# A feed forward block computed plainly in two of its four blocks and by Strassen's algorithm in the others

## Chip, core and metric

The kernel runs on one core of a Trainium2 chip. The metric is the device time of one execution in microseconds; the median of three runs before the change is 1663.09 us (1661.41 to 1663.12).

## What is computed

One inference step of a two-layer recurrent decoder over 576 tokens (512 of a prompt, 64 of samples), width 1024. Each layer has a mixer, a feed forward and a gated embedding:

```python
for i in range(DEPTH):                       # 2 layers
    hn = rmsnorm(h, prm['norm_mix'][i])
    ...                                      # layer 0: mLSTM and retention; layer 1: HGRN2 and S5
    h = h + out
    hn = rmsnorm(h, prm['norm_ff'][i])
    h = h + jnp.matmul(jnp.square(jax.nn.relu(jnp.matmul(hn, prm['w_ff1'][i]))), prm['w_ff2'][i])
    gate = jax.nn.sigmoid(jnp.matmul(rmsnorm(h, prm['norm_ple'][i]), prm['w_ple_gate'][i]))
    h = h + gate * jnp.matmul(p[i], prm['w_ple_proj'][i])
```

The feed forward goes from 1024 to 4096 features and back. The state space model (S5) of the second layer needs constants that depend on its parameters alone: powers of its poles, turned phases, and products of these with its input and output matrices. They can be made at any time before the second layer.

## The kernel before

Features lie on the 128 partitions and the 576 tokens along the free dimension, in two halves of 288 columns (HALF). All matrices are float32. TensorE takes each product in three: a value is split into a high part (rounded to fp32r) and a low part (the rest), and high x high, high x low and low x high are added in PSUM. So a weight of 128 x 128 against 576 tokens takes six matmuls of 288 columns. `unit` loads eight such weights (512 KB) by SP's queue, ScalarE copies the high part (L238) and VectorE subtracts it for the low part (L239); the raw, high and low tiles have two buffers each. `cols` runs the 48 matmuls of one unit into a PSUM bank pair, of which three rotate (`pb`, L250).

`ff` is the feed forward, once for each layer. It goes over four blocks of 1024 hidden features. In a block, the first product (called FF1 below) takes eight units; each result is scaled and cut at zero by VectorE (`fu`, L562) and squared by ScalarE (L563). The second product, from the block's 1024 features to all 1024 outputs, is done with Strassen's algorithm: `seven` takes two outputs n and n+1 and the two token halves as a 2 x 2 problem and makes seven products of 4 x 3 = 12 matmuls in place of eight (L519), so 84 matmuls for each of four pairs. `seven_in` makes the sums of u that this needs (seven splits of 288 columns and four sums for each pair of u), `seven_weights` the sums of weights (four sums, L493 to L501, and seven splits of 512 columns, L480 and L481). Two PSUM banks accumulate on through several products: after each product VectorE adds the bank as it stands to h (L524), and the next product into that bank has to wait for this.

In the first feed forward alone, `s5_hooks` hangs the work on the constants of S5 beside the loop. `hook(b, part, n)` runs what is planned for block b, first (0) or second (1) product, step n. The tables (`s5_tables`, many small VectorE instructions on 128 x 32 to 128 x 288) come from (0,0,4) on. Then come 24 steps, three for each of eight sets of four groups: `elem` (six multiplications and additions on VectorE, L1263 to L1265, with two loads of s5bc), `prod` (four transposes, L1277, and four products, L1279, on TensorE, then small DMAs to DRAM) and `s5_turn` (some 40 small VectorE instructions on s5R, then stores of s5R and s5M). s5R and the product tile s5t of `elem` share one buffer. The first step stands at (0,1,6), the last at (3,1,0). All run at a lowered priority (`LATE`).

The order of each engine's queue is not that of the code: a planner with a timeline model places the instructions in the order of priority as their inputs and buffers come free. The engines then run their queues in that fixed order.

Of the kernel before, what the change touches and what calls it, by code (L numbers as in the profile page):

```python
# [10 lines left out]
F32R = mybir.dt.float32r  # L11
AF = mybir.ActivationFunctionType
ALU = mybir.AluOpType
# [3 lines left out]
P = 128  # L17
# [3 lines left out]
HALF = NT // 2  # L21
# [8 lines left out]
LOP = "fqig"  # L30
MAGIC = 12582912.0
LATE = 100

# [140 lines left out]
class K:  # L176
# [364 lines left out]
    def ff(self, l, hooks=None):  # L541
        nc = self.nc
        xs, r = self.norm(f"ff{l}")
        with ExitStack() as st:
            pool = lambda name, bufs: st.enter_context(self.tc.tile_pool(name=f"{name}{l}", bufs=bufs))

            ap, fw = pool("fa", 3), pool("fw", 1)
            todo = hooks(st) if hooks else {}
            up = pool("ff", 4)

            def hook(*at):
                if at in todo:
                    todo[at]()

            for b in range(4):
                us, pair = [], []
                for n in range(8):
                    hook(b, 0, n)
                    w = self.unit("col", "w_ff1", l, (8 * b + n) * P, 0)
                    ps = self.cols(w, xs)  # L560
                    u = self.np_.tile([P, NT], F32, name="fu", tag=("sqa", "sq")[n % 2])
                    nc.vector.scalar_tensor_tensor(self.sv(u), self.pv(ps), 0.0, self.sv(r()), ALU.max, ALU.mult)  # L562
                    nc.scalar.activation(u, u, AF.Square)  # L563
                    if n % 2 == 0:
                        pair = [u]
                        parts = self.seven_in(pair, up, ap)
                        us.append(next(parts))
                    else:
                        pair.append(u)
                        next(parts)  # L570
                if b == 3 and l == 1:
                    self.embed_in(l, self.np_, nc.sync, self.xp, "sq")
                for n in range(0, 8, 2):
                    hook(b, 1, n)
                    hook(b, 1, n + 1)
                    self.seven(l, n, b, us, fw)


    def ple(self, l):
# [646 lines left out]
    def s5_hooks(self, st):  # L1226


        nc = self.nc
# [70 lines left out]
        def late(f, *at):  # L1300

            def run():
                with self.tc.high_priority(-LATE):
                    f()
            old = hooks.get(at)
            hooks[at] = run if old is None else lambda: (old(), run())

        for j in range(4, 13):
            late(piece, 0, j // 8, j % 8)
        late(lambda: piece(99), 0, 1, 5)  # L1310
        at = lambda i: (i // 16, i // 8 % 2, i % 8)
        steps = [lambda f=f, ct=ct, q=q: f(ct, q) for ct in range(4) for q in range(2)
                 for f in (elem, prod, lambda ct, q: self.s5_turn(sp, ct, q))]
        for i, f in enumerate(steps):
            late(f, *at(14 + i * 44 // len(steps)))
        return hooks


# [421 lines left out]
```

## Time and profile before

| | |
|---|---|
| median of three runs | 1663.09 us |
| the profiled execution, its own time | 1658.75 us |
| its span, first to last instruction | 1656.5 us |
| TensorE (PE) busy | 1563.3 us, 94% |
| VectorE (DVE) busy | 1261.0 us, 76% |
| ScalarE (ACT) busy | 718.1 us, 43% |
| GpSimd (POOL) busy | 214.5 us, 13% |

The trace is of one execution. PE counts matmuls, PEld weight loads, which overlap them; a matmul's end is modelled, so that neighbours overlap and the pace is read from starts. [...] A row of waits names who waited, for whom, the sum in us, the number of waits and the longest. In a row of the timeline the number in brackets is the engine's idle time just before, and what ended it. In a row of instruction groups the numbers behind the bar are busy us in all, mean ns of one, and idle us before them.

### The profile page before, as it was taken

The page shows a single profiled execution, that of the slowest core. Times are in us where ns is not written, and L with a number is a line of the kernel's source. Part 1 is how long each engine was busy: PE and PEld are TensorE (multiplying, and loading weights), DVE is VectorE, ACT ScalarE, POOL GpSimd, SP SyncE. Part 2 cuts the span into 40 slices and gives each one's busy share as a digit, 9 for nine tenths or more (in the row PEclk, how much of TensorE's full clock was granted, in tenths as well). Part 3 has the DMA queues.
Part 4 walks back from the last instruction along what each step waited for, and adds up shares of the span by engine and source line. Part 5 has one row for each costly group of instructions (what it writes and reads, how often), then busy time and mean ns, then how long its engine had stood idle before and what let it go on. Part 6 is the DMA issues. An engine that isn't in the chain of part 4 may idle for free.

```text
span 1656.5 us, 30820 instructions
## 1 busy us (share of the span) xinstructions
PE 1563.3 (94%) x12213; PEld 1502.4 (91%) x12213; DVE 1261.0 (76%) x2745; ACT 718.1 (43%) x1326; POOL 214.5 (13%) x204
## 2 busy tenths in 40 slices
PE   7999999999999999999899788989999999999896
PEld 6989789999999899899899787979999999999895
DVE  6977666658998988989685896386777785867855
ACT  4333222335534435345453356374543534435553
POOL 1311122201000000000023465231100000000000
PEclk9999999999999999999999899899999999999998
DMA  7222222223232333332326422521223222222221
GB/s 266 99 91 81 94 78 92 82 95 103 71 120 97 103 129 103 120 121 84 133 91 179 142 93 79 153 87 70 89 77 115 77 75 96 81 95 91 90 77 58
DMA packets 83311, 168.83 MB, mean 102 GB/s; under 512 B 33760, under 2 KB 40800, under 8 KB 83040
## 3 DMA queue, kind: packets, MB, share of 16 engines
q1 hardware_dynamic: 81512, 163.40, 29.9%
q8 instruction: 96, 1.57, 0.4%
q0 software_dynamic: 640, 2.36, 0.4%
q10 hardware_dynamic: 1016, 1.11, 0.2%
q14 instruction: 47, 0.39, 0.1%
HBM read 142.70 MB, written 24.13 MB: 101 GB/s over the span
## 4 chain that ended last, share of the span: by engine, by line
PE 71%; DVE 17%; DMA 4%; ACT 3%; issue 3%; SPq 1%; POOL 0%; DVEq 0%; ACTq 0%
PE pb L250 49%; PE pb L519 13%; PE pm L519 2%; DMA wr<-in_w_dram 2%; DVE h L524 1%; DVE wl L239 1%; DVE wsl L481 1%; DVE xl L286 1%; DVE wl L481 1%; PE pm L653 1%; DVE ul L283 1%; PE pm L1005 1%; DVE e L1526 1%; PE pm L891 1%; DMA sG<-Gd 1%
## 5 line engine op out<-in xcount | busy, mean ns | idle before, releaser
L250 PE MATMUL pb<-xh,wh 128*128 128x288 f32 x2480 | 550.8, 301 | 28.4 <-ACT xh L282 6.3
L250 PE MATMUL pb<-xh,wl 128*128 128x288 f32 x2480 | 547.5, 299 | 0.5 <-DVE wl L239 0.5
L250 PE MATMUL pb<-xl,wh 128*128 128x288 f32 x2480 | 547.6, 299 | 0.1
L250 PEld LDWEIGHTS pb<-xh,wh 128*128 128x128 f32 x2480 | 406.8, 191 | 36.7 <-issue 10.7
L250 PEld LDWEIGHTS pb<-xl,wh 128*128 128x128 f32 x2480 | 406.9, 191 | 7.8 <-issue 7.0
L250 PEld LDWEIGHTS pb<-xh,wl 128*128 128x128 f32 x2480 | 406.5, 191 | 6.0 <-issue 4.8
L238 ACT CAST wh<-wr 128x1024 fp32r<-128x1024 f32 x155 | 162.2, 1048 | 312.4 <-PE pb L250 254.4
L239 DVE TENSOR_TENSOR wl<-wr,wh 128x1024 fp32r<-128x1024 f32 x135 | 166.1, 1231 | 28.2 <-ACT wh L238 25.0
L519 PE MATMUL pb<-uh,wsh 128*128 128x288 f32 x512 | 154.7, 302 | 12.9 <-DVE h L524 9.9
L519 PE MATMUL pb<-ul,wsh 128*128 128x288 f32 x512 | 152.1, 297 | 0.0
L519 PE MATMUL pb<-uh,wsl 128*128 128x288 f32 x512 | 151.0, 297 | 0.0
L480 ACT CAST wsh<-wsum 128x512 fp32r<-128x512 f32 x128 | 78.9, 619 | 145.0 <-PE pb L519 99.2
L519 PEld LDWEIGHTS pb<-uh,wsh 128*128 128x128 f32 x512 | 96.8, 189 | 19.3 <-DVE h L524 11.1
L524 DVE TENSOR_TENSOR h<-h,pb 128x288 f32<-128x288 f32 x192 | 85.2, 447 | 32.1 <-PE pb L519 31.5
L519 PEld LDWEIGHTS pb<-ul,wsh 128*128 128x128 f32 x512 | 96.9, 189 | 0.0
L519 PEld LDWEIGHTS pb<-uh,wsl 128*128 128x128 f32 x512 | 96.7, 190 | 0.0
L481 DVE TENSOR_TENSOR wsl<-wsum,wsh 128x512 fp32r<-128x512 f32 x128 | 87.4, 683 | 2.3 <-ACT wsh L480 1.1
L562 DVE SCALAR_TENSOR_TENSOR fu<-pb,r 128x576 f32<-128x576 f32 x64 | 48.1, 753 | 46.0 <-PE pb L250 45.9
L282 ACT CAST uh<-ut 128x288 fp32r<-128x288 f32 x128 | 52.6, 431 | 45.2 <-DVE ut L453 24.9
L411 POOL TENSOR_TENSOR sqa<-sqa,sq 128x576 f32<-128x576 f32 x3 | 5.1, 1714 | 441.7 <-ACT sq L410 441.7
L239 POOL TENSOR_TENSOR wl<-wr,wh 128x1024 fp32r<-128x1024 f32 x20 | 50.5, 2529 | 90.2 <-ACT wh L238 88.6
L1507 POOL MEMSET W<- 128x576 f32 x4 | 2.3, 576 | 429.5 <-PE pb L519 428.1
(495 smaller groups left out, 2563.2 us busy)
## 6 DMA issues: line engine op xcount, KB each, us to landing
wr<-in_w_dram SPq DMA_DIRECT2D x219, 512.0 KB, 3.7
sR<-Rd SPq DMA_DIRECT2D x12, 256.0 KB, 2.9
h<-in_hT_dram SPq DMA_DIRECT2D x8, 288.0 KB, 5.2
prd<-po POOLq DMA_DIRECT2D x8, 288.0 KB, 3.2
Gd<-s5G SPq DMA_DIRECT2D x8, 288.0 KB, 3.8
prj<-prd SPq DMA_DIRECT2D x8, 288.0 KB, 4.6
sG<-Gd SPq DMA_DIRECT2D x8, 288.0 KB, 5.4
s_in<-in_Cst_dram SPq DMA_DIRECT2D x4, 516.0 KB, 7.9
```

Source lines behind the costliest of these rows:

```text
L238: nc.scalar.copy(hi, raw)
L239: (nc.gpsimd if self.lo_pool else nc.vector).tensor_tensor(lo, raw, hi.bitcast(F32), ALU.subtract)
L250: mm(ps[:, j if bank is None else bank, :HALF], a, b[:, j * HALF:(j + 1) * HALF], start=first and a is wh and b is xh, stop=last and a is wl)
L282: nc.scalar.copy(hi, src)
L283: nc.vector.tensor_tensor(lo, src, hi.bitcast(F32), ALU.subtract)
L286: nc.vector.scalar_tensor_tensor(lo, src, scale, hi.bitcast(F32), ALU.mult, ALU.subtract)
L480: nc.scalar.copy(hi, src)
L481: nc.vector.tensor_tensor(lo, src, hi.bitcast(F32), ALU.subtract)
L519: mm(ps, a[:, k], x[:, i], start=start and k == 0 and a is wh and x is xh, stop=k == 3 and a is wl, skip_group_check=not start)
L524: nc.vector.tensor_tensor(o, o, ps, ALU.add)
L562: nc.vector.scalar_tensor_tensor(self.sv(u), self.pv(ps), 0.0, self.sv(r()), ALU.max, ALU.mult)
L653: nc.tensor.transpose(dst, src[:n, t0:t0 + tn], self.ident[:n, :n])
```

## The change

The first feed forward takes two kinds of blocks. In the first two (NPLAIN) the second product is done plainly: u is split whole (576 columns) as the inputs of the first product are, `w_ff2` is taken in eight units of 48 matmuls by `cols`, and VectorE adds each result to its h whole. The two other blocks, and the second feed forward, keep Strassen's algorithm. The 24 steps of the constants are hung closer: over 21 steps of the loop instead of 44, from (0,1,6) to (2,0,2).

```diff
+NPLAIN = 2
...
             for b in range(4):
                 us, pair = [], []
+                plain = l == 0 and b < NPLAIN
...
                     nc.scalar.activation(u, u, AF.Square)
-                    if n % 2 == 0:
+                    if plain:
+                        if n % 2 == 0:
+                            hi, lo = (up.tile([P, 7, HALF], F32R, name=t, tag=t) for t in ("uh", "ul"))
+                        f = lambda t: t[:, n % 2 * 2:n % 2 * 2 + 2].rearrange("p a b -> p (a b)")
+                        us.append((f(hi), f(lo)))
+                        self.split_into(*us[-1], u)
+                    elif n % 2 == 0:
                         pair = [u]
...
                     hook(b, 1, n + 1)
-                    self.seven(l, n, b, us, fw)
+                    if not plain:
+                        self.seven(l, n, b, us, fw)
+                        continue
+                    for m in (n, n + 1):
+                        w = self.unit("col", "w_ff2", l, m * P, 8 * b)
+                        ps = self.cols(w, us)
+                        nc.vector.tensor_tensor(self.sv(self.h[m]), self.sv(self.h[m]), self.pv(ps), ALU.add)
...
-            late(f, *at(14 + i * 44 // len(steps)))
+            late(f, *at(14 + i * 21 // len(steps)))
```

Lines of the changed kernel stand 1 to 14 further down (L250 is L251, L1277 is L1291, L1264 is L1278, L1218 is L1232; the plain product's add is L590).

TensorE's queue where the first block's second product begins, before. `uh`, `ul` are the parts of u, `wh`, `wl` those of the weights, `pb` and `pm` PSUM banks:

```order
L250 MATMUL pb<-xl,wh 128x288 x2
L250 MATMUL pb<-xh,wl 128x288 x2
L519 MATMUL pb<-uh,wh 128x288
L519 MATMUL pb<-ul,wh 128x288
L519 MATMUL pm<-uh,wh 128x288
L519 MATMUL pm<-ul,wh 128x288
L519 MATMUL pb<-uh,wl 128x288
```

The same place now:

```order
L251 MATMUL pb<-xl,wh 128x288 x2
L251 MATMUL pb<-xh,wl 128x288 x2
L251 MATMUL pb<-uh,wh 128x288 x2
L251 MATMUL pb<-ul,wh 128x288 x2
L251 MATMUL pb<-uh,wl 128x288 x2
```

Two Strassen products that shared the engine (pb and pm) have given way to the first product's own form, both halves for each weight.

VectorE's queue in the second block's second product, before, from the end of a turn (L1218 writes s5R last) to the next `elem` (L1264 writes s5t into the same buffer once s5R is stored):

```order
L1218 TENSOR_SCALAR s5R<-s5R 64x256
L524 TENSOR_TENSOR h_123<-h_123,pb 128x288
L495 TENSOR_TENSOR wsum<-wsum,wr_6556 128x512
L524 TENSOR_TENSOR h_121<-h_121,pb 128x288
L481 TENSOR_TENSOR wsl<-wsum,wsh 128x512
L1264 TENSOR_TENSOR s5t<-s5bc,s5y_5001 128x4x128
L498 TENSOR_TENSOR wsum<-wr_6556,wsum 128x512
L1265 TENSOR_TENSOR s5ET<-s5ET,s5t 128x512
```

Such a place now, in the same product:

```order
L1232 TENSOR_SCALAR s5R<-s5R 64x256
L590 TENSOR_TENSOR h_121<-h_121,pb 128x576
L240 TENSOR_TENSOR wl<-wr_6557,wh 128x1024
L1278 TENSOR_TENSOR s5t<-s5bc,s5y_4929 128x4x128
L1279 TENSOR_TENSOR s5ET<-s5ET,s5t 128x512
L1277 TENSOR_TENSOR s5G<-s5bc,s5w_4922 128x576
L590 TENSOR_TENSOR h_122<-h_122,pb 128x576
L1278 TENSOR_TENSOR s5t<-s5bc,s5w_4923 128x576
L240 TENSOR_TENSOR wl<-wr_6613,wh 128x1024
```

Between the end of a turn and the `elem` that takes its buffer stand two instructions in place of four, and the weight splits of the plain units stand behind.

TensorE's queue at a set of constants in FF1, before (the last of the eight sets):

```order
L250 MATMUL pb<-xl,wh 128x288
L1277 MATMUL pm<-cc,s5ET 128x128
L250 MATMUL pb<-xl,wh 128x288
L1277 MATMUL pm<-cc,s5ET 128x128
L250 MATMUL pb<-xh,wl 128x288
L1277 MATMUL pm<-cc,s5ET 128x128
L250 MATMUL pb<-xh,wl 128x288
L1277 MATMUL pm<-cc,s5ET 128x128
L250 MATMUL pb<-xh,wh 128x288
L1279 MATMUL pm<-s5G,s5ET 16x128
```

The last set now, in FF1 of the third block:

```order
L251 MATMUL pb<-xh,wl 128x288 x2
L251 MATMUL pb<-xh,wh 128x288 x2
L1291 MATMUL pm<-cc,s5ET 128x128 x4
L251 MATMUL pb<-xl,wh 128x288 x2
L251 MATMUL pb<-xh,wl 128x288 x2
```

Four transposes that each stood between two matmuls stand together; their four products (L1293) follow together too, 16 rows on. Of the eight sets, three now stand so; before, one stood together whole, and two with transposes alone.

## Rows read from the trace of the kernel before

**Rows 1.** The page: span, and busy time of each engine.

```profile
span 1656.5 us, 30820 instructions
...
PE 1563.3 (94%) x12213; PEld 1502.4 (91%) x12213; DVE 1261.0 (76%) x2745; ACT 718.1 (43%) x1326; POOL 214.5 (13%) x204
```

**Rows 2.** Windows, feed forward 1: length, PE, PEld, DVE, ACT, POOL busy (count), clock

```profile
388.60:439.40 50.80, 50.74 (x389) 50.77 (x390) 48.12 (x175) 28.99 (x52) 0.84 (x1) 1.00 0.35 95
388.60:504.80 116.20, 111.97 (x821) 109.25 (x822) 110.03 (x385) 50.95 (x92) 0.84 (x1) 0.99 0.33 100
504.80:612.10 107.30, 105.70 (x767) 100.37 (x766) 95.22 (x266) 44.81 (x84) 0.00 (x0) 1.00 0.34 111
612.10:722.60 110.50, 106.47 (x779) 101.75 (x779) 98.54 (x275) 48.39 (x94) 0.00 (x0) 1.00 0.35 111
722.60:819.80 97.20, 91.78 (x667) 88.27 (x665) 79.97 (x188) 45.65 (x84) 0.78 (x3) 1.00 0.28 93
```

**Rows 3.** Windows of feed forward 2: whole, a middle block, the last part.

```profile
1178.20:1575.70 397.50, 390.24 (x2908) 387.12 (x2908) 297.00 (x553) 177.65 (x311) 0.00 (x0) 1.00 0.26 88
1326.80:1423.40 96.60, 96.05 (x723) 95.82 (x722) 70.64 (x132) 40.82 (x72) 0.00 (x0) 1.00 0.26 88
1520.10:1575.70 55.60, 50.08 (x362) 47.92 (x360) 46.64 (x87) 27.29 (x46) 0.00 (x0) 1.00 0.23 79
```

**Rows 4.** Waits of PE, feed forward 1: total us, times, longest us.

```profile
PE pb L519 <- DVE h L524: 7.3, 14, 1.3
PE pb L519 <- ACT wh L480: 2.6, 4, 0.9
```

**Rows 5.** Windows of line L250 alone: length, PE, PEld busy (count), clock.

```profile
400.00:436.00 36.00, 36.00 (x280) 36.00 (x279) 1.00 0.35 95
1390.00:1420.00 30.00, 30.00 (x227) 30.00 (x226) 1.00 0.26 88
```

**Rows 6.** The constants on PE: windows of L1277 (four), then of L1279.

```profile
388.60:504.80 116.20, 0.60 (x4) 0.49 (x4) 0.99 0.33 100
504.80:612.10 107.30, 2.60 (x12) 1.61 (x12) 1.00 0.34 111
612.10:722.60 110.50, 2.61 (x12) 1.61 (x12) 1.00 0.35 111
722.60:819.80 97.20, 1.00 (x4) 0.57 (x4) 1.00 0.28 93
388.60:504.80 116.20, 0.41 (x8) 0.13 (x8) 0.99 0.33 100
504.80:612.10 107.30, 3.84 (x24) 1.12 (x24) 1.00 0.34 111
612.10:722.60 110.50, 3.26 (x25) 0.91 (x24) 1.00 0.35 111
722.60:819.80 97.20, 1.57 (x8) 0.44 (x8) 1.00 0.28 93
```

**Rows 7.** A window, and PE's timeline there: start, us, instruction.

```profile
453.50:456.90 3.40, 3.40 (x15) 3.40 (x16) 2.94 (x9) 0.62 (x1) 0.00 (x0) 0.51 0.00 0
453.33 0.45 PE L519 MATMUL pb<-uh,wsh 128*128 128x288 f32 x1 [1.34 <-DVE h L524]
453.57 0.45 PE L519 MATMUL pb<-ul,wsh 128*128 128x288 f32 x1
```

**Rows 8.** The page: costliest groups, those of a unit's weights and of u.

```profile
L238 ACT CAST wh<-wr 128x1024 fp32r<-128x1024 f32 x155 | 162.2, 1048 | 312.4 <-PE pb L250 254.4
L239 DVE TENSOR_TENSOR wl<-wr,wh 128x1024 fp32r<-128x1024 f32 x135 | 166.1, 1231 | 28.2 <-ACT wh L238 25.0
L562 DVE SCALAR_TENSOR_TENSOR fu<-pb,r 128x576 f32<-128x576 f32 x64 | 48.1, 753 | 46.0 <-PE pb L250 45.9
```

**Rows 9.** Waits of DVE, feed forward 1, for the store of s5R.

```profile
DVE s5t L1264 <- DMA Rd<-s5R: 4.5, 2, 2.8
```

**Rows 10.** The page: loads of weights, us from issue to landing.

```profile
wr<-in_w_dram SPq DMA_DIRECT2D x219, 512.0 KB, 3.7
```

## Prediction

> **What bounds the kernel now.** I read the page's first section, then windows over the stretch that the change touches, then TensorE's waits, then the prices of single instructions. TensorE is busy 1563.3 of 1656.5 us [rows 1], so an edit pays only as far as it shortens or lengthens TensorE's own queue. The stretch is the first feed forward, 388.6 to 819.8 us. Cut where the last Strassen product of each block ends, its four blocks take 116.2, 107.3, 110.5 and 97.2 us [rows 2]; up to 90 matmuls of the next block's first product are drawn in ahead of such an end, so I count matmuls by window. The second feed forward runs the same Strassen loop without the constants, and there a block takes 96.6 us [rows 3]. The reader is to see two things: VectorE is busy 110.0 of 116.2 us in the first block against 70.6 of 96.6 in the second feed forward, and TensorE's waits in the first feed forward end mostly with VectorE's adds to h (7.3 us in 14 waits) and with ScalarE's copies of Strassen's weights (2.6 us in 4) [rows 4].
>
> To split a block's time I need the matmul's pace. A window of 30.0 us without a wait counts 227 matmuls, two of which began before it: 0.1335 us each. In the first block's first product the pace is quicker, 36.0/278 = 0.130 us [rows 5].
>
> Block time = matmuls x 0.1335 + the constants' own TensorE time + the rest, which is waits, restarts after them and half clock. Counts are those of rows 2 less two at the edge and less the constants' instructions; the constants' time is the sum of their two lines [rows 6].
> - Block 0: 116.2 - 807 x 0.1335 (107.7) - 1.0 = 7.5. Since some 320 matmuls ran at 0.130 (1.1 us gained), the waits are really 8.6.
> - Block 1: 107.3 - 729 x 0.1335 (97.3) - 6.4 = 3.6.
> - Block 2: 110.5 - 741 x 0.1335 (98.9) - 5.9 = 5.7.
> - Block 3: 97.2 - 653 x 0.1335 (87.2) - 2.6 = 7.4.
> - Second feed forward, a middle block: 96.6 - 721 x 0.1335 (96.25) = 0.35; its last part, 1520.1 to 1575.7: 55.6 - 360 x 0.1335 (48.1) = 7.5 [rows 3].
>
> So the end of the last block loses 7.4 us with the constants and 7.5 without. That loss is Strassen's own, and stays.
>
> **The change part by part.** *More matmuls.* A plain block's second product takes 8 x 8 x 6 = 384 matmuls, Strassen's 4 x 7 x 12 = 336. Two blocks add 96: 96 x 0.1335 = +12.8 us, all on TensorE, which nothing hides.
>
> [...]
>
> *Waits that go, blocks 0 and 1.* Strassen's products share two accumulating banks, and a product must wait until VectorE has added the bank's last state to h; its weights need four sums and seven splits per pair. Both are what rows 4 name, and the plain product has neither: it takes three rotating banks and two weight splits per pair, as the first product does. The first product of block 0 ran beside the constants' tables with VectorE busy 48.1 of 50.8 us, and TensorE was busy 50.7 of them [rows 2]: this form did not wait at 95% VectorE. After the change VectorE has less to do: per plain block 16 splits of 1.23 us and 24 instructions of 0.75 us [rows 8], 37.7 us, against 70.6. Tables and constants cost VectorE roughly what the two feed forwards differ by, about 87 us (110.0 + 95.2 + 98.5 + 80.0 = 383.8 [rows 2] against 297.0 [rows 3]); two plain blocks with all of it make 162 of some 217 us, 75%. The first Strassen block after them gets nothing but its own 70.6. At the turn from first to second product the last u is wanted 42 matmuls, 5.6 us, after the first product ends, and four instructions of about 0.75 us make it. So I take 8.6 + 3.6 = 12.2 us as gone. [...] What is late next is TensorE itself.
>
> *Waits that go, block 2.* All constants now stand before the first Strassen product (VectorE's last three rows of them lie among that block's first weight sums), so block 2 becomes a block of the second feed forward: 5.7 - 0.35 = 5.3 us gone. Block 3 keeps its 7.4.
>
> *The constants on TensorE move.* The same 96 records (rows 6: 6.8 + 9.1 = 15.9 us). Where a set of four transposes and four products stands together, it took 1.0 us (block 0's one set); where matmuls of the first product stand between all of them, 2.6 (block 3's one set: transposes 1.0, products 1.6 in four pieces, 0.4 a piece). In the new order three of eight sets stand together, two have transposes apart and products nearly together (1.0 + 0.8), three have transposes apart and products in three pieces (1.0 + 1.2): 3 x 1.0 + 2 x 1.8 + 3 x 2.2 = 13.2, so 2.7 us less. Lower bound of the gain 0, since the pairing may matter less than the durations say; I take 2.0.
>
> *What is packed closer.* Each of the eight turns of constants ends with a store from s5R, and the next elem step needs that buffer. VectorE works in the order of its queue: it stood 4.5 us behind this store in two of eight cases, 2.8 us the longest [rows 9]. In the new order only none to five short instructions lie between, so seven waits of 1 to 3 us are likely. Behind the waiting instruction stand the next weight split, u or add, and TensorE waits for those. The cover: a unit lasts 48 x 0.1335 = 6.4 us and its weights are double buffered, so a copy of 1.05 and a split of 1.23 [rows 8] leave 4.1 us. 2.8 fits under it, and 75% load lets VectorE catch up. SP's queue now carries the constants' DMAs between weight loads, but raw weights are fetched almost two units ahead and land 3.7 us after issue [rows 10]. Bounds: 0 (as in the first product before) to the 12.2 us of waits that stood in these blocks; I take 2.0, near the first, since the row of the same form showed none. Also, block 0's second product may keep the pace of 0.130 us (384 x 0.0035 = 1.3 us); not counted, kept for the low end.
>
> **Sum.** +12.8 - 12.2 - 5.3 - 2.0 + 2.0 = -4.7 us against the profiled execution of 1658.75 us (span 1656.5 and 2.25 around it): 1654.0. The median of the runs, 1663.09, lies 4.3 us above that execution, and the forecast is given against the median: 1658.4 us.
>
> **The rivals.**
> - *An even trade.* Half of the old waits of blocks 0 and 1 come back as waits behind the packed constants: 6.1 instead of 2.0. For it: the constants' steps now come every 2.5 units or so, and VectorE cannot pass a waiting instruction. Against: rows 2's first products without a wait. Sum -0.6: 1662.5 us.
> - *Slower.* The store of s5R holds VectorE beyond the 4.1 us of cover, because the wait of up to 2.8 us adds to the constants' own 3 to 4 us ahead of the same split; then TensorE waits in nearly every one of the seven turns, and what blocks 0 and 1 lost before they lose again: +12.8 - 5.3 - 2.0 = +5.5 us, 1668.6. It decides from the point where wait plus queued constants exceed 4.1 us over a unit's own 2 to 3 us of VectorE work. [...]
> - *The move does not happen,* since the steps are given at a lowered priority and a planner places them. The order excludes it: the last set of constants on TensorE stands 96 rows ahead of the first Strassen product. No chance given.
>
> **How the numbers follow.** Forecast 0.60, even trade 0.28, slower 0.12. About 0.2%, 3.3 us, is what a measurement of this kernel can tell from no change. The forecast's own range runs from -8.7 (no new wait, 2.7 and 1.3 gained) to about -3: 1654.4 to 1660; a small part of it, 0.04, lies within 0.2%. So faster 0.56, same 0.33, slower 0.11. The range for 8 in 10 takes in the forecast, the even trade and the start of the third: 1654.5 to 1666.
>
> **What would show it.** Matmuls of the plain second product at 0.130 to 0.134 us with next to no wait in blocks 0 and 1; block 0, its 768 matmuls, near 103 us, block 1 near 112 with six sets of constants in it, block 2 with a loss under 1 us; no half clock between 400 and 600 us; VectorE at about 75% in blocks 0 and 1; the constants' two lines near 13 to 14 us on TensorE. Wrong would be: waits of TensorE behind weight splits L240 in block 1 beside long VectorE waits for the store of s5R, or a first Strassen block that still loses 5 us though no constants stand in it.

## The result, and the profile after

The changed kernel takes 1648.64 us in the median (1644.37 to 1650.61, 4 runs) against 1662.25 us (1658.43 to 1663.12) for the kernel before beside it: a ratio of 0.9917, 95% interval 0.9901 to 0.9933. A second set gave 1648.67 against 1662.42 us, 0.9917 (0.9904 to 0.9931). Faster was forecast, 1658.4 us with a range of 1654.5 to 1666; the gain, 13.6 us, is nearly three times the 4.7 of the sum, and the range does not hold it. One execution of the last kernel under Experiments took 4602.64 us; its ratio leaves this one out.

The page after: span, then busy time of each engine; beside [rows 1], TensorE as long busy in a span 8 us shorter, VectorE 49 us less.

```profile
span 1648.5 us, 30745 instructions
...
PE 1563.2 (95%) x12309; PEld 1508.3 (91%) x12309; DVE 1212.0 (74%) x2561; ACT 690.8 (42%) x1246; POOL 211.9 (13%) x204
```

Windows of the first feed forward after, cut where each block's second product ends, the whole last; columns as in [rows 2] (the clock is the granted share of TensorE's full clock), then the busy share of the DMA engines and GB/s.

```profile
388.50:490.50 102.00, 102.00 (x775) 102.00 (x776) 76.14 (x292) 32.89 (x43) 0.82 (x1) 1.00 0.34 101
490.50:602.40 111.90, 111.90 (x840) 106.87 (x839) 86.12 (x272) 36.33 (x63) 0.00 (x0) 1.00 0.43 137
602.40:712.50 110.10, 109.32 (x825) 107.87 (x825) 90.21 (x224) 47.57 (x87) 0.00 (x0) 1.00 0.32 108
712.50:809.60 97.10, 93.69 (x691) 92.02 (x690) 74.23 (x140) 46.17 (x81) 0.80 (x3) 1.00 0.22 77
388.50:809.60 421.10, 416.90 (x3125) 408.76 (x3125) 326.70 (x925) 162.96 (x272) 1.62 (x4) 1.00 0.33 107
```

The stretch falls from 431.2 us (388.6 to 819.8, [rows 2]) to 421.1. In the two plain blocks TensorE shows no idle time; VectorE is busy 76.1 of 102.0 us, 75% as reckoned. The granted clock is 1.00 throughout, with no stretch like that of [rows 7], where matmuls started 0.24 us apart at 0.51 granted.

Who waits in the stretch after: first TensorE's waits, then the longest of VectorE's (us in all, times, longest).

```profile
PE pb L520 <- DVE h L525: 2.8, 4, 1.0
PE pb L251 <- DVE s5pi L1124: 0.9, 1, 0.9
PE pb L251 <- ACT xh L286: 0.9, 1, 0.9
PE pb L520 <- ACT wh L481: 0.2, 1, 0.2
...
DVE h L590 <- PE pb L251: 26.7, 13, 4.7
DVE fu L564 <- PE pb L251: 20.0, 19, 3.0
...
DVE s5t L1278 <- DMA Rd<-s5R: 3.2, 2, 2.5
```

Of [rows 4]'s 7.3 us in 14 waits for adds to h, 2.8 in 4 are left, all in the Strassen blocks; the waits for weight copies went from 2.6 to 0.2. The plain blocks have no wait but one of 0.9 at the feed forward's start, which stood there before too; the other 0.9 is the wait for xh behind the last Strassen block. VectorE now waits for TensorE: its adds L590 stood 26.7 us until a product was there. Behind the store of s5R it stood 3.2 us in two waits.

The constants' two lines on TensorE after, L1291 (transposes) and L1293 (their products), over the stretch.

```profile
388.50:809.60 421.10, 6.87 (x32) 4.29 (x32) 1.00 0.33 107
388.50:809.60 421.10, 6.38 (x64) 1.88 (x64) 1.00 0.33 107
```

13.25 us, against 15.9 [rows 6].

To compare kernels I took the start of every matmul from the first of this feed forward to the 49th of the stage after it (48 of them are drawn in among the last Strassen products). Matmuls count 0.1335 us each; a *loss* is the idle time in front of a matmul with the late start that follows it; *constants* is what the starts around a set are late beyond the pace; the remainder is clock and pace.

| | stretch | matmuls | losses | constants | remainder |
|---|---|---|---|---|---|
| before | 431.1 | 391.4 | 19.4 | 16.1 | 4.2 |
| before, second trace | 431.7 | 391.4 | 20.1 | 16.0 | 4.2 |
| after | 421.1 | 404.2 | 5.7 | 12.0 | -0.7 |
| after, second trace | 420.6 | 404.2 | 5.2 | 12.0 | -0.9 |

The matmuls cost the +12.8 of the prediction; the three other columns give back 13.7, 4.1 and 4.9 in the first pair: -10.0, and -11.2 in the second. Of the 4.9, the half clock of [rows 7] was about 1.5, an estimate: 14 starts in 3.4 us, where the pace makes 1.9. The rest of the difference of the medians lies outside the stretch and is less certain. The profiled executions of the second pair took 1664.89 and 1651.0 us, 2.5 and 2.3 above 1662.42 and 1648.67. Of their 13.9 us, 11.2 are the stretch, 2.6 the second feed forward, about 1 the part after it, and the part between lost 1.0; in the first pair the second feed forward gained 1.3 and the part between lost 4.0. The gain of the second feed forward is no scatter. With Strassen's third sum in pm it takes 395.9 to 396.1 us in all seven traces with two or four plain blocks, and 397.4 to 399.0 in the four with none or one. The queues of TensorE, VectorE and ScalarE hold the same instructions there in the same order before and after, so the order is not the reason; what is stays open.

### The profile page after: what moved, and what is told of

Its sections match the earlier page's. It is cut to its first block, busy times and chain, and to the rows that moved or that the text cites. A ratio compares the mean times of both kernels' runs of the same rounds, so it can differ in the third digit from the quotient of the medians.

```text
span 1648.5 us, 30745 instructions
## 1 busy us (share of the span) xinstructions
PE 1563.2 (95%) x12309; PEld 1508.3 (91%) x12309; DVE 1212.0 (74%) x2561; ACT 690.8 (42%) x1246; POOL 211.9 (13%) x204
## 3 DMA queue, kind: packets, MB, share of 16 engines
q10 hardware_dynamic: 1016, 1.11, 0.2%
## 4 chain that ended last, share of the span: by engine, by line
PE 74%; DVE 14%; ACT 4%; DMA 4%; issue 3%; SPq 1%; POOL 0%; DVEq 0%; ACTq 0%; POOLq 0%
PE pb L251 54%; PE pb L520 11%; PE pm L520 2%; DMA wr<-in_w_dram 1%; DVE wl L240 1%; DVE xl L287 1%; PE pm L667 1%; DVE h L525 1%; PE pm L905 1%; PE pm L1019 1%; DVE e L1540 1%; ACT hsq L936 1%; PE pm L927 1%; ACT wh L239 0%; DVE st L293 0%
## 5 line engine op out<-in xcount | busy, mean ns | idle before, releaser
L251 PE MATMUL pb<-xh,wh 128*128 128x288 f32 x2480 | 549.1, 300 | 33.1 <-DVE z L1492 7.5
L251 PE MATMUL pb<-xh,wl 128*128 128x288 f32 x2480 | 547.0, 299 | 0.5 <-DVE wl L240 0.5
L251 PE MATMUL pb<-xl,wh 128*128 128x288 f32 x2480 | 546.2, 299 | 0.1
L251 PEld LDWEIGHTS pb<-xh,wh 128*128 128x128 f32 x2480 | 406.2, 191 | 41.3 <-issue 16.5
L251 PEld LDWEIGHTS pb<-xl,wh 128*128 128x128 f32 x2480 | 406.0, 191 | 6.9 <-issue 6.1
L251 PEld LDWEIGHTS pb<-xh,wl 128*128 128x128 f32 x2480 | 406.3, 191 | 6.6 <-issue 5.5
L520 PE MATMUL pb<-uh,wsh 128*128 128x288 f32 x384 | 114.2, 297 | 4.8 <-DVE h L525 4.2
L520 PE MATMUL pb<-ul,wsh 128*128 128x288 f32 x384 | 113.5, 296 | 0.0
L520 PE MATMUL pb<-uh,wsl 128*128 128x288 f32 x384 | 113.2, 295 | 0.0
L481 ACT CAST wsh<-wsum 128x512 fp32r<-128x512 f32 x96 | 59.2, 619 | 106.1 <-PE pb L520 75.2
L525 DVE TENSOR_TENSOR h<-h,pb 128x288 f32<-128x288 f32 x144 | 64.2, 448 | 37.3 <-PE pb L520 37.2
L520 PEld LDWEIGHTS pb<-uh,wsh 128*128 128x128 f32 x384 | 72.1, 188 | 7.2 <-DVE h L525 4.5
L520 PEld LDWEIGHTS pb<-ul,wsh 128*128 128x128 f32 x384 | 72.1, 188 | 0.0
L520 PEld LDWEIGHTS pb<-uh,wsl 128*128 128x128 f32 x384 | 72.1, 188 | 0.0
L482 DVE TENSOR_TENSOR wsl<-wsum,wsh 128x512 fp32r<-128x512 f32 x96 | 65.7, 685 | 2.8 <-ACT wsh L481 1.5
L251 PE MATMUL pb<-ul,wh 128*128 128x288 f32 x256 | 55.2, 297 | 0.0
```

Source lines behind the costliest of these rows:

```text
L251: mm(ps[:, j if bank is None else bank, :HALF], a, b[:, j * HALF:(j + 1) * HALF], start=first and a is wh and b is xh, stop=last and a is wl)
L481: nc.scalar.copy(hi, src)
L482: nc.vector.tensor_tensor(lo, src, hi.bitcast(F32), ALU.subtract)
L520: mm(ps, a[:, k], x[:, i], start=start and k == 0 and a is wh and x is xh, stop=k == 3 and a is wl, skip_group_check=not start)
L525: nc.vector.tensor_tensor(o, o, ps, ALU.add)
```

## Experiments

Each ratio is against the kernel before, run beside it. The table has the account above, in us; *third sum* is the bank of a Strassen pair's third accumulator. The letters of the theories hold within a group of runs, not from one group to the next.

| plain blocks | steps | third sum | median us | ratio, interval | stretch | losses | constants |
|---|---|---|---|---|---|---|---|
| 0 | 44 | pm | 1662.4 | before | 431.1 | 19.4 | 16.1 |
| 2 | 44 | pm | 1656.0 | 0.9961 (0.9947-0.9975) | 429.0 | 7.4 | 16.1 |
| 0 | 21 | pm | 1687.5 | 1.0145 (1.013-1.0161) | 454.9 | 47.4 | 11.7 |
| 1 | 21 | pm | 1676.4 | 1.0078 (1.0061-1.0096) | 445.6 | 30.9 | 14.1 |
| 2 | 21 | pm | 1648.7 | 0.9917 (0.9904-0.9931) | 421.1 | 5.7 | 12.0 |
| 2 | 16 | pm | 1647.2 | 0.9908 (0.9889-0.9928) | 419.1 | 5.9 | 9.3 |
| 2 | 10 | pm | 1646.3 | 0.990 (0.9879-0.992) | 418.5 | 5.8 | 8.3 |
| 4 | 21 | pm | 1659.3 | 0.9982 (0.9966-0.9997) | 427.6 | 0.0 | 11.9 |
| 0 | 44 | pb | 1661.7 | 0.9988 (0.9977-0.9999) | 430.4 | 19.4 | 16.3 |
| 0 | 21 | pb | 1653.4 | 0.9942 (0.993-0.9955) | 424.6 | 21.0 | 8.7 |
| 0 | 10 | pb | 1653.4 | 0.9939 (0.9918-0.996) | 424.3 | 19.3 | 8.7 |
| 1 | 21 | pb | 1648.1 | 0.9913 (0.9899-0.9926) | 420.9 | 10.0 | 11.4 |
| 1 | 10 | pb | 1646.0 | 0.9903 (0.9881-0.9926) | 417.3 | 9.8 | 8.4 |

### Both kernels again

> The kernel before once more, for a second trace of it. Theory A: the first feed forward takes 430 to 432 us again, with 18 to 24 us of waits, restarts and half clock, and the stretches outside it scatter by 2 to 4 us from execution to execution. Theory B: the stretches outside differ from the changed kernel's by more than they differ between two executions of the same kernel.

> The changed kernel once more, for a second trace and more times. Theory A (all of the gain is made in the first feed forward, by waits of TensorE that are gone there and constants that stand closer together): the first feed forward takes 421 us again, against 431 before, and the rest of the program what it took before within some 2 us, so the times differ by about 10 us, a ratio near 0.994. Theory B (a part of the 13.6 us between the medians is made outside that stretch): the ratio stays near 0.992 and the stretches outside are together 3 to 4 us shorter than in the traces of before.

1664.65 us for the kernel before, a ratio to itself of 1.0004 (0.999 to 1.0018), and 1648.67 us for the changed one. The second set gives the gain of the first; executions of one kernel scatter by 3 to 13 us, so a single trace tells its stretch better than its span.

### One half of the change at a time

The plain blocks alone, the constants as before:

```diff
-            late(f, *at(14 + i * 21 // len(steps)))
+            late(f, *at(14 + i * 44 // len(steps)))
```

> The two plain blocks alone; the constants stay spread over 44 steps of the loop, so about half of them stand beside Strassen blocks. Theory A: blocks 0 and 1 lose nothing more, +12.8 - 12.2 us, but block 2 keeps about 5 us of waits and two to four sets of constants stay apart: 0 to 3 us faster than before, ratio 0.998 to 1.000. Rival C (the plain blocks bring the gain, wherever the constants stand): 8 to 10 us faster, ratio 0.994.

The closer steps alone: in the kernel before, the reverse edit.

> The packing alone; all four blocks stay Strassen's and the constants stand within 21 steps. Theory A: VectorE then has 2 x 70.6 + 87 = 228 us of work in two blocks that take TensorE about 2 x 96 + 13 = 205 us, so it becomes the bound there: blocks 0 and 1 lose 20 us or more where they lost 12, blocks 2 and 3 gain 5 to 8: 0 to 15 us slower than before, ratio 1.000 to 1.009. Rival D (packing brings the gain, the plain products only cost): 5 us or more faster, ratio 0.997 or less.

The plain blocks alone gain 6.5 us, a ratio of 0.9961 that lies between those of the two theories: the losses fall from 19.4 to 7.4, the constants stay at 16.1. By the prediction's method, which counts in half clock and late starts, block 2 still loses 5.1 us in this trace, as theory A had it (1.4 with the closer steps too), so the closer steps pay in block 2 besides what they give on the constants' lines. The closer steps alone lose 25 us, more than either theory had. Together the halves gain 13.8: the closer steps pay only beside the plain blocks. TensorE's first waits with the closer steps alone:

```profile
PE pm L1277 <- DVE s5ET L1265: 20.1, 2, 10.6
PE pb L519 <- DVE h L524: 8.2, 12, 2.0
PE pm L1279 <- DVE s5G L1265: 4.8, 2, 2.5
```

TensorE stood twice for 10 us at the constants' own transposes. No such row stands in [rows 4], and none of the prediction's terms or rivals has TensorE wait there.

### How close, and how many plain blocks

The changed kernel with the steps over 16 and over 10 (`i * 16`, `i * 10`), with `NPLAIN = 1` and with `NPLAIN = 4`:

> The changed kernel with the 24 steps of the constants over 16 steps of the loop in place of 21. What it tells apart is where VectorE's cover ends. Worked from the traces: seven sets of constants cost VectorE some 8.8 us each (the 61.9 us by which the first feed forward's last three blocks differed from Strassen's own before, over seven sets), 62 us, and stand in 16 units of 6.4 us, 102 us, beside some 38 us of the plain block's own work: about 98% of VectorE's time. Theory A (nothing waits as long as VectorE has room, and the constants are cheaper on TensorE the more of a set stands together: six of eight sets now, three before): the constants' two lines take 11 us instead of 13.3 on TensorE, no new wait, 1646 to 1649 us against 1648.7 for the changed kernel. Theory B (the wait for the store of s5R reaches TensorE as soon as the turns stand closer): seven waits of 1 to 3 us behind weight splits, 1655 us or more.

> The changed kernel with the 24 steps over 10 steps of the loop. 62 us of constants and some 24 us of the loop's own work then stand in about 65 us of TensorE's time: VectorE is asked for 132%. Theory A (the room on VectorE decides): TensorE waits for roughly the excess, 10 to 20 us in block 1, less 3 us from sets that all stand together: 1656 to 1666 us, with waits of TensorE behind the weight split L240. Theory C (the planner gives the loop's own work the way, and the constants only drift later, so that closeness costs nothing): 1645 to 1650 us.

> The changed kernel with one plain block in place of two, constants over 21 steps as in the changed kernel. 48 matmuls fewer, 6.4 us. Theory A (two plain blocks are wanted for the room on VectorE): block 1's Strassen products now run beside three to four sets of constants, VectorE is asked for some 95 to 100% there, and 5 to 15 us of TensorE's waits come back: 1648 to 1657 us. Theory D (it is the first block, beside the tables, that needs the room; the second plain block buys little): 1642 to 1646 us.

> The changed kernel with all four blocks of the first feed forward plain. 96 more matmuls, 12.8 us. Blocks 2 and 3 of the changed kernel still lose about 1.5 and 5.3 us to Strassen's own waits. Theory A (a plain block has next to no wait, and the last block's loss is Strassen's own): 12.8 less some 5.5 us, 1654 to 1657 us. Theory E (the last block's loss belongs to the end of the feed forward and comes with either form): 12.8 less 1.5, 1660 us.

With two plain blocks closeness costs nothing: over 16 and 10 steps the losses stay at 5.9 and 5.8, and the constants fall to 9.3 and 8.3, as the sets stand together. The medians, 1647.2 and 1646.3, are 1.5 and 2.4 us lower, which their intervals cannot tell from the changed kernel. Over 10 steps the estimate of 132% for VectorE should have cost 10 to 20 us by theory A; theory C was right. The last set, hung at the end of the second block's first product (its second product begins at 547.5), runs on TensorE only at 623.6, the last start in this row of L1291:

```profile
L1291 PE MATMUL pm<-cc,s5ET x32: 270/272/273, 491.5 to 623.6; 128*128 128x128 f32 x32
```

With one plain block the same 21 steps cost 28 us more than with two, and 1676.4 us is 19 above the upper end of theory A. Its TensorE in the second block's second product, a timeline (start, us, instruction, idle before and what ended it), and VectorE's timeline there:

```profile
576.52 0.29 PE L520 MATMUL pb<-uh,wal 128*128 128x288 f32 x1
587.16 1.09 PE L1291 MATMUL pm<-cc,s5ET 128*128 128x128 f32 x4 [10.35 <-DVE s5ET L1279]
590.79 0.58 PE L1293 MATMUL pm<-s5G,s5ET 128*16 128x128 f32 x2 [2.54 <-DVE s5G L1279]
591.31 0.61 PE L520 MATMUL pm<-uh,wh 128*128 128x288 f32 x1
...
582.69 0.28 DVE L1232 TENSOR_SCALAR s5R<-s5R 64x256 f32<-64x256 f32 x1
585.60 0.69 DVE L1278 TENSOR_TENSOR s5t<-s5bc,s5y 128x512 f32<-128x512 f32 x1 [2.63 <-DMA Rd<-s5R]
586.33 0.69 DVE L1279 TENSOR_TENSOR s5ET<-s5ET,s5t 128x512 f32<-128x512 f32 x1
```

Read from below: VectorE ends a turn, waits 2.63 us for the store of s5R, makes s5ET, and only then TensorE goes on, after 10.35 us. The store is what the prediction's rival *slower* named, but it is a quarter of the 10.35 us; most of the rest is VectorE's work on the turn before it. And it reaches TensorE by another way: not a weight split stands behind it, but the set itself, and behind the set a Strassen product into one of the banks pm, at 591.31. Nothing of the 576 tokens' work ran on TensorE between 576.8 and 587.2.

With four plain blocks the stretch has no loss at all, as theory A said, and the last block's loss goes with Strassen. The time does not agree with it: 10.7 us above the changed kernel, near theory E's 1660, though E's reason, a loss at the end, is not in the trace. The trace shows 6.5 us more in the stretch (12.8 for matmuls, less 5.7 and 0.7) and a wait of 3.3 just ahead of it where the changed kernel waits 0.9; it ends with an instruction of the tables (L1098 on s5p), so tables stood in VectorE's queue ahead of the feed forward's start. The traced execution, 1654.91 us, lies 4.4 below this kernel's median, so the 10.7 are not all accounted for. The wait:

```profile
PE pb L251 <- DVE s5p L1098: 3.3, 1, 3.3
```

### The two banks

PSUM has three bank pairs pb and two banks pm here. A set of constants takes both banks pm, a Strassen pair takes one for its third accumulator, and a buffer goes round in the order of the code. So a Strassen product cannot have its bank until the set that stands ahead of it in the code has been made and read, and the lowered priority of the constants is of no use. The plain product takes no pm. So the code reads; to test it, Strassen's third accumulator was moved, at the price of one more pair pb for each Strassen pair:

```diff
-        pa, pc, pb = ac[:, 0, :HALF], ac[:, 1, :HALF], self.pmt()[:, :HALF]
+        pa, pc, pb = ac[:, 0, :HALF], ac[:, 1, :HALF], self.bulk()[:, 0, :HALF]
```

> No plain block, the constants over 21 steps (the kernel that took 1687.5 us), with one edit: the third accumulator of a Strassen pair comes from the banks pb in place of pm, so that the two banks pm belong to the constants alone in the feed forward. Theory A (buffer order: the two banks pm go round in the order of the code, so a Strassen product that takes one has to wait for the set of constants that stands ahead of it in the code, however late VectorE makes it): the waits of TensorE of about 10 us before the constants' transposes go, the waits of the first feed forward fall from 47 us to under 22, and the time to 1645 to 1665 us. Theory V (VectorE has not the time: busy 385 us of the stretch): the waits move to the weight sums and stay above 35 us, 1675 us or more. The second feed forward, which has no constants, shows what the edit costs Strassen itself: 0 to 3 us.

> One plain block and the constants over 21 steps (the kernel that took 1676.4 us), with the third accumulator of a Strassen pair from pb. Theory A: the 10.4 us wait before the transposes and the 3.4 before their products go; 1645 to 1657 us. Theory V: 1670 us or more.

> The kernel before (no plain block, constants over 44 steps) with the same edit: the third accumulator from pb. Theory A: of the 19 to 20 us of waits in the first feed forward some 5 to 8 go, those in which a product waited behind constants, and the rest, Strassen's own, stays: 1652 to 1658 us. Theory V: waits as before, 1660 to 1665 us.

Over 21 steps the edit gives back 34 us without a plain block (1687.5 to 1653.4) and 28 us with one (1676.4 to 1648.1): theory A. TensorE's waits without a plain block now:

```profile
PE pb L520 <- ACT wh L481: 6.8, 8, 1.8
PE pb L520 <- DVE h L525: 4.7, 8, 0.9
PE pb L520 <- DVE wl L482: 2.5, 5, 1.0
PE pm L1291 <- DVE s5ET L1279: 1.5, 1, 1.5
```

The 20.1 us at the transposes have become 1.5. VectorE had no more room than before: 383.5 us busy of 424.6 (90%), with the closer steps alone 387.6 of 454.9. The transposes could drift instead, their last start at 726.1 us against 673.2, though the loop ended 28 us earlier. Windows of the stretch, closer steps alone and then with the moved bank:

```profile
388.60:843.50 454.90, 412.34 (x3029) 398.24 (x3029) 387.58 (x1109) 189.86 (x352) 1.66 (x4) 0.97 0.31 99
...
390.90:815.50 424.60, 407.57 (x3029) 396.73 (x3029) 383.54 (x1109) 189.88 (x352) 1.57 (x4) 1.00 0.34 106
```

The edit costs Strassen itself nothing that shows: the second feed forward, all Strassen, takes 396.6 to 398.7 us in five kernels with it, against 397.4 to 399.0 in the four traces without it that have none or one plain block.

Over 44 steps the edit does next to nothing: 1661.7 us, a gain of 1.0 (the interval, to 0.9999, only just leaves out none), losses 19.4 as before, theory V. So the 19 us that the kernel before lost are not the banks' doing; they are Strassen's own waits beside a loaded VectorE, as the prediction said, and the second row of the table (the plain blocks alone) shows that it is the plain product that takes them away. The banks matter once the steps stand close.

The reverse, the changed kernel with every second plain unit in pm:

```diff
+                        if m % 2:
+                            pq = [self.pmt() for _ in range(2)]
...
+                            for j in range(2):
+                                o = self.h[m][:, j * HALF:(j + 1) * HALF]
+                                nc.vector.tensor_tensor(o, o, pq[j][:, :HALF], ALU.add)
+                            continue
                         ps = self.cols(w, us)
```

> The reverse: the changed kernel (two plain blocks, 21 steps), where every second unit of the plain second product accumulates in the two banks pm in place of a pair pb, 48 matmuls as before; VectorE adds it in two halves, 8 more instructions of some 0.45 us against 0.75 for each two. Theory A: a unit then has to wait for the constants that stand ahead of it in the code, and they can't drift: TensorE waits at the constants (L1291, L1293 as they are named in the changed kernel) or at these units for 5 to 20 us in all in blocks 0 and 1, 1654 to 1670 us. Theory V (with VectorE at 75% there is room, whatever the order): 1648 to 1651 us.

1650.67 us, ratio 0.9924 (0.9911 to 0.9938); the stretch takes 425.1 us, 4.0 to 4.5 more than after, of which 3.8 are losses (9.4). The time is in theory V's range and out of theory A's; at the median 2 us are lost. The sign and the place are A's, but the waits that came back in blocks 0 and 1, 4.5 us in the rows below, stay under its 5. So sharing the banks is not dear by itself: it cost 34 us where VectorE was busy 85% of the stretch (387.6 of 454.9) and came late with the constants, and 2 to 4 us beside two plain blocks, where every second unit shares them. The rows (L1303 are the transposes, L1291 VectorE's last step for them):

```profile
PE pm L1303 <- DVE s5ET L1291: 1.8, 1, 1.8
PE pb L251 <- ACT wh L239: 1.7, 2, 0.9
PE pb L251 <- DVE wl L240: 1.0, 2, 0.5
```

### What plain blocks buy beyond the banks

> No plain block, Strassen's third accumulator from pb, constants over 10 steps. Theory A (the shared banks were the whole price of closeness): the constants drift as VectorE finds room, as over 21 steps, 1650 to 1655 us (over 21 steps: 1653.4). Theory V (plain blocks are wanted for room on VectorE once the steps are this close): waits of TensorE well above the 21 us measured over 21 steps, 1658 us or more.

> One plain block, the third accumulator from pb, constants over 10 steps. Theory A: 48 matmuls (6.4 us) fewer than with two plain blocks, against some 5 us more of Strassen's waits; sets of constants together (8 to 9 us on TensorE, not 11.4): 1643 to 1647 us. Theory V: the waits of block 1 take more than the 6.4 us back: 1650 us or more.

With Strassen off pm, none, one and (from above, without that edit) two plain blocks over 10 steps take 1653.4, 1646.0 and 1646.3 us. The first block brings its losses' worth (19.3 to 9.8 us, for 6.4 of matmuls; clock and pace give another 3.7): 7 us. The second brings 4.0 and 1.0 of clock and pace for 6.4, so nothing. Both runs came out where theory A had them. The first block's 7 us point to room on VectorE beside the tables, as theory D of the run with one plain block had it; no run shows that room apart from the form of the product.

The last run makes the last block of the second feed forward plain too:

```diff
-                plain = l == 0 and b < NPLAIN
+                plain = l == 0 and b < NPLAIN or l == 1 and b == 3
```

> As own1_10, and the last block of the second feed forward plain too: 48 matmuls more (6.4 us) against the 7.5 us that this block loses at its end. If that loss is Strassen's own it goes whole, as it did in the first feed forward with four plain blocks (no wait left): 0 to 1.5 us faster than own1_10. If it belongs to the end of the feed forward, 4 to 6 us slower.

TensorE's waits in the second feed forward, first without, then with the plain last block:

```profile
PE pb L520 <- DVE h L525: 4.1, 8, 1.0
PE pb L520 <- DVE wl L482: 0.9, 2, 0.7
PE pb L251 <- ACT wh L239: 0.9, 1, 0.9
PE pb L520 <- ACT wh L481: 0.7, 2, 0.5
...
PE pb L520 <- DVE h L525: 1.0, 3, 0.3
PE pb L251 <- ACT wh L239: 0.9, 1, 0.9
PE pb L520 <- DVE wl L482: 0.2, 1, 0.2
```

The loss at the end goes with Strassen's form: the waits fall from 6.6 us in these rows to 2.1. From the start of this feed forward to the end of the program it is 1.5 us shorter (477.8 to 476.3). The median, 1644.72 us, ratio 0.9884 (0.9852 to 0.9916), is the lowest of all kernels here and 0.2% below the changed kernel's; from the run without this edit, 1645.98, it cannot be told apart.

## Why the prediction missed

The direction was right, and so were the causes of the gain that it named. Two terms failed: block 3, put at 0 because its loss "is Strassen's own, and stays", gave 2.3 us, and the new waits, put at +2.0, were none. The prediction's low end, -8.7, already had no new wait, the whole gain on the constants and a quicker second product; what put the stretch below it is block 3. The other 3.5 us of the median's 13.6 lie outside the stretch, where the prediction had no term. By the prediction's own method (matmuls x 0.1335 and the constants' lines taken from each window), the four blocks lose now -1.5, -1.1, 1.4 and 5.1 us, against 7.5, 3.6, 5.7 and 7.4:

| term | forecast | measured |
|---|---|---|
| 96 matmuls | +12.8 | +12.8 |
| blocks 0 and 1: waits gone | -12.2 | -13.7, both rows together |
| new waits behind the store of s5R | +2.0 | in the row above |
| block 2 | -5.3 | -4.3 |
| block 3 | 0 | -2.3 |
| constants on TensorE | -2.0 | -2.6 |
| sum | -4.7 | -10.1 |

- **More matmuls.** Right. Block 0 took 102.0 us, near the 103 forecast, block 1 111.9, near 112. In blocks 0 and 1 starts came a little quicker than 0.1335 (0.1315 and 0.1320 us, the windows after less the constants' instructions): that is the negative loss, and the 1.3 us of a quicker second product that the prediction kept for the low end; it came about whole.
- **New waits, +2.0.** A step that failed: 10.2 expected from the two blocks in balance, 13.7 found, of which 1.5 are the quicker starts and 2.0 this term. The prediction expected seven waits of 1 to 3 us behind the store of s5R, bounded their cost between 0 and 12.2 and took 2.0. VectorE stood there twice, 3.2 us in all, and TensorE has no wait in these blocks for it: VectorE is ahead of it (the 26.7 us of waits for products). The lower bound was the value.
- **Rivals.** The *even trade* did not come about. *Slower* was a real mechanism with the wrong place. The store of s5R does hold VectorE 2.6 us, as a part of the 10.35 us that TensorE stood at one place, and waits of this size stand in the first feed forward only where a Strassen product waits for the same bank pm, with none or one plain block. The prediction read neither the shared banks nor that the plain product keeps off them; so it had no such reason to exclude the rival, and gave it and the even trade 0.40.
- **Block 2, -5.3.** Mostly right: 1.4 us are still lost where 0.35 was forecast, one wait of 0.5 for an add to h and one of 0.2 for a copy.
- **Block 3, 0.** The 7.4 us were taken over unchanged as Strassen's own. This step failed. They are Strassen's own (the trace with four plain blocks has none of it), but not fixed: 5.1 us are left. TensorE's waits in this block, before and then after (the wait for xh is the start of the next stage):

```profile
PE pb L519 <- DVE h L524: 2.1, 4, 0.7
PE pb L250 <- ACT xh L285: 0.9, 1, 0.9
PE pb L519 <- DVE wl L481: 0.9, 1, 0.9
PE pb L519 <- ACT wh L480: 0.8, 1, 0.8
PE pb L519 <- ACT wsh L480: 0.6, 1, 0.6
...
PE pb L520 <- DVE h L525: 2.2, 3, 1.0
PE pb L251 <- ACT xh L286: 0.9, 1, 0.9
PE pb L520 <- DVE wl L482: 0.2, 1, 0.2
```

  The waits for the adds are the same 2.1 and 2.2 us; what went are those for weight splits and copies, 2.3 us down to 0.2. That the constants left this block (VectorE 80.0 us busy before, 74.2 after) is not the reason: with the plain blocks alone two sets still stand in it, VectorE is busy 82.8 of 101.9 us, and it loses 5.0 us as well, with no wait for a split or a copy. Its window, and TensorE's waits there:

```profile
713.60:815.50 101.90, 98.59 (x714) 93.98 (x712) 82.83 (x189) 49.24 (x91) 0.80 (x3) 1.00 0.28 91
...
PE pb L520 <- DVE h L525: 2.3, 4, 0.7
PE pb L251 <- ACT xh L286: 0.9, 1, 0.9
```

  The end of the second feed forward, which the prediction took for its measure, moved too: 7.6 us before and 6.6 after, counted from the last 361 starts, in queues that did not change. The cause of both stays open.
- **Constants, -2.0.** The reckoned 2.7 came about, 2.6 by the lines' busy time; the cut to 2.0 was needless caution. By starts, where what matmuls lose beside them is counted, it is 4.1. With the steps over 10, seven of eight sets stand together, and the lines take 8.9 us, 1.11 a set.
- **Median.** The forecast took 4.7 us off the median, as if nothing else moved. The stretch gave 10.0 to 11.2; of the rest of 13.6, 1.3 to 2.6 are the second feed forward's, which comes with the plain blocks for a reason that stays open, and what is left no trace settles.

## What to carry to other kernels

Low-priority work drifted here only as far as its buffers let it (last transposes at 673.2 us with the banks shared, at 726.1 with banks of their own): where it shared a rotating set of PSUM banks with the main loop, the order of the code was the order of the engine, so look at who else takes from the pool before pricing such a move. What the sharing cost went with how late the low-priority work came: 34 us without a plain block, 2 to 4 beside two. When two loads share an engine, a costlier form of the one (14% more matmuls in a block's second product) can pay if it takes less of the shared engine; once the banks were apart, one block beside the heaviest load bought 7 us, the second nothing. VectorE's 26.7 us of waits for the plain blocks' products stood beside no idle time of TensorE there, so ask first who is ahead.

## What was not expected

- A shared pair of banks cost 34 us, 2% of the program, with the closer steps alone, and nothing with the steps of the kernel before: it shows as TensorE waiting for VectorE at the small product, with the big one behind it.
- VectorE at 90% of the stretch, with constants free to drift and four Strassen blocks, goes with 21 us of losses; at 78% (two plain blocks over 10 steps, 327.1 of 418.5) with 5.8, all in the Strassen blocks. The share alone does not set it: the first product did not wait at 95% [rows 2]. The window:

```profile
389.20:807.70 418.50, 414.13 (x3124) 408.51 (x3124) 327.13 (x925) 163.05 (x272) 1.54 (x4) 1.00 0.33 107
```

- Eight small f32 instructions among fp32r matmuls cost 2.0 us a set net of the pace in the kernel before, where one of eight sets stands together (16.1 over eight), and 1.0 with the steps over 10, where seven do (8.3).
